# Mixture-of-experts layers: 32 slots for each of four experts side by side in TensorE's array, with a conditional block for ranks 32 to 63

## The chip, the cores and the metric

The kernel runs on one core of a Trainium2 chip, as one launch. The metric is the device time of that launch in microseconds, the median of several runs. A profile is one execution of the same program, taken by the hardware profiler.

## The reference, cut to what matters

The program is a DeltaNet layer and a product-key expert layer (the first block), then a second block of two layers. Each of the two layers is a token mixer followed by a mixture of experts. All of it is float32 on 256 tokens of 1024 channels. Only the mixture of experts is touched here. With `N_EXPERTS` = 32, `D_EXPERT` = 256 and `TOP_K` = 2 it is:

```python
def hierarchical_moe(h, w_grp, b_grp, w_exp, b_exp, w_gate, w_up, w_down):
    ...
    combine = jnp.einsum('tk,tke->te', weights,
                         jax.nn.one_hot(expert_id, N_EXPERTS, dtype=jnp.float32)).astype(t.dtype)
    y = jnp.zeros_like(t)
    for gi in range(N_GROUPS):
        sl = slice(gi * EXPERTS_PER_GROUP, (gi + 1) * EXPERTS_PER_GROUP)
        hid = jax.nn.silu(jnp.einsum('td,edf->tef', t, w_gate[sl])) * jnp.einsum('td,edf->tef', t, w_up[sl])
        y = y + jnp.einsum('tef,efd->td', hid * combine[:, sl, None], w_down[sl])
    return y.reshape(b, l, d)
```

A token goes to two of the eight experts of one group, so that 512 pairs of token and expert are spread over 32 experts. The reference evaluated on its inputs spreads them unevenly. In quads of four neighbouring experts, the fullest expert of each quad has 41, 35, 14, 11, 28, 31, 14 and 18 tokens in the first of the two layers, and 28, 25, 22, 30, 21, 12, 15 and 23 in the second.

## The kernel before, in words

`moe` (called once a layer) normalises the tokens, routes them and computes for each token and expert a rank `R`: the number of earlier tokens that chose the same expert, or a negative number where the token did not choose it. `cnt` holds the number of tokens of each expert. `moe_round` then computes all 32 experts for the tokens of ranks 0 to 63. If an expert had more than 64 tokens, a loop at the end of `moe` (L1793 to L1797) would run `moe_round` again with `R` lowered by 64.

`moe_round` works by pairs of experts (p = 0 to 15), 64 slots for each:

- `dispatch(q)`, once for each four experts: VectorE builds the selection matrix `sel` (256 tokens by 4 x 64 slots) from `R`, and TensorE multiplies the tokens (split into a high and a low part, `xh` and `xl`) with it (L1893, L1894), 32 matmuls of 256 columns. ScalarE and VectorE move the result to `xe`.
- `gate_up(p, k0)`: gate and up projection of the pair in one PSUM bank `pg`, L1914. Each of the two experts occupies 64 of the array's 128 columns, and streams its own weights `wgu` (512 columns).
- `turn(p)`: transposes of `sel` and of the hidden values `hs` (L1928, L1930).
- `down(p)`: the down projection with the weights `wdn` (L1946) into the banks `pw`, again two experts side by side; then the gate of the layer (L1951) and the split into `dsh` and `dsl` (L1952, L1953).
- `scatter(p)`: adds the pair to the tokens' accumulators `macc` (L1959).

The loop at the end of `moe_round` lays these out as a software pipeline: between the two halves of `gate_up(p)` comes `turn(p - 1)`, and `scatter(p - 2)` and `down(p - 1)` follow. TensorE takes its instructions in the order in which the tile library's scheduler put them, and so does each other engine.

The weights are the bulk of the traffic. An expert has four `wgu` tiles and two `wdn` tiles of 512 KB each. There is room for six experts (`units`, pools `mw` and `mw2`). Experts 0 to 3 are loaded during the token mixer, 4 and 5 at the start of `moe` (L1748), and the other 26 by SyncE's queue from inside the round (L1874): each load waits there, in order, until the matmuls that read the buffer's last content are done, and until the eighth load before it has landed.

The lines of the round:

Of the kernel before, what the change touches and what calls it, by code (L numbers as in the profile page):

```python
# [33 lines left out]
class Ker:  # L34
# [1229 lines left out]
    def units(self, e, part):  # L1264


        pool = self.mw2 if e % 6 > 3 or self.again else self.mw
        n = 2 if part else 4
        r = []
        for u in range(n):  # L1270
            for j in range(2):
                if part:
                    t = pool.tile([128, D], F32, name="wdn", bufs=8 if pool is self.mw else 4)
                    src = self.a["w2_d"][self.layer, e + j][:, u, :]
                else:
                    t = pool.tile([128, 2, 512], F32, name="wgu", bufs=16 if pool is self.mw else 8)
                    src = self.a["w2_gu"][self.layer, e + j][:, 2 * u:2 * u + 2, :]
                self.wt[e + j, part, u] = t
                yield t[:], src

# [456 lines left out]
    def moe(self, l):  # L1737
# [44 lines left out]
        self.moe_round(l, xh, xl, R, W, gc, sh, wk, 6, weights)  # L1782

        mx = sp.tile([128, 1], F32, name="mx")
        nr = sp.tile([128, 1], mybir.dt.int32, name="nr")
        nc.vector.tensor_reduce(mx[:], cnt[:], mybir.AxisListType.X, ALU.max)
        nc.vector.tensor_scalar(mx[:], mx[:], -1.0, None, ALU.add)
        nc.vector.tensor_copy(nr[:], mx[:])
        nc.vector.tensor_scalar(nr[:], nr[:], 6, None, ALU.arith_shift_right)
# [3 lines left out]
        n = nc.values_load(nr[0:1, 0:1], min_val=0, max_val=3)  # L1793
        with tc.For_i(0, n, 1):  # L1794
            nc.vector.tensor_scalar(R[:], R[:], -64.0, None, ALU.add)
            self.again = True
            self.moe_round(l, xh, xl, R, W, gc, sh, wk, 0)  # L1797
# [56 lines left out]
    def moe_round(self, l, xh, xl, R, W, gc, sh, wk, loaded, weights=None):  # L1854
# [9 lines left out]
        iota = self.sm("iota")[:, 0:64].unsqueeze(1).to_broadcast([128, 4, 64])  # L1864
        wt = self.wt

        room = 2 if self.again else 6
        ahead = [self.units(e, part) for e in range(loaded, room, 2) for part in range(2)]
        xe, sel, wsl, sT, hT, ds, hs, gu, nxt = [{} for _ in range(9)]
        bank = lambda: pw.tile([128, 512], F32, name="pw")  # L1870

        def load(n, it):
            for u in itertools.islice(it, n):
                nc.sync.dma_start(*u)  # L1874

        def later(e, part):
            return self.units(e, part) if e < 32 else iter(())

        def dispatch(q):

            sel[q] = wk.tile([128, 2, 4, 64], F32R, name="sel")
            for i in range(2):
                nc.vector.tensor_tensor(sel[q][:, i], iota, R[:, i, 4 * q:4 * q + 4].unsqueeze(2).to_broadcast([128, 4, 64]),
                                        ALU.is_equal)
            if weights and q == 0:
                weights()
            xe[q] = xp.tile([128, KC, 256], F32, name="xe")
            for k in range(KC):
                ps = bank()
                ks = slice(k * 128, (k + 1) * 128)  # L1890
                for i in range(2):
                    r = sel[q][:, i].rearrange("p e s -> p (e s)")
                    mm(ps[:, 0:256], xh[:, i, ks], r, start=i == 0, stop=False)  # L1893
                    mm(ps[:, 0:256], xl[:, i, ks], r, start=False, stop=i == 1)  # L1894
                if k % 2:
                    nc.scalar.activation(xe[q][:, k, :], ps[:, 0:256], AF.Identity, bias=sh[:, k:k + 1], scale=gc[:, k:k + 1])
                else:
                    nc.vector.tensor_scalar(xe[q][:, k, :], ps[:, 0:256], gc[:, k:k + 1], sh[:, k:k + 1], ALU.mult, ALU.add)
            ps = bank()
            for e in range(4):  # L1900
                for i in range(2):
                    mm(ps[e % 2 * 64:e % 2 * 64 + 64, e // 2:e // 2 + 1], sel[q][:, i, e, :].bitcast(F32),
                       W[:, i, 4 * q + e:4 * q + e + 1], start=i == 0, stop=i == 1)
            wsl[q] = wk.tile([128, 2], F32, name="wsl")
            nc.vector.tensor_copy(wsl[q][:], ps[:, 0:2])

        def gate_up(p, k0):
            if k0 == 0:
                nxt[p] = later(2 * p + room, 0)
                gu[p] = pg.tile([128, 512], F32, name="pg")  # L1910
            for k in range(k0, k0 + 4):
                for j in range(2):
                    s0 = (p % 2 * 2 + j) * 64
                    mm(gu[p][j * 64:j * 64 + 64, :], xe[p // 2][:, k, s0:s0 + 64], wt[2 * p + j, 0, k // 2][:, k % 2, :],  # L1914
                       start=k == 0, stop=k == KC - 1)
                if k % 2:
                    load(2, nxt[p])
            if k0:
                hs[p] = wk.tile([128, 256], F32, name="hs", bufs=1)
                nc.scalar.activation(hs[p][:], gu[p][:, 0:256], AF.Silu)  # L1920
                nc.vector.scalar_tensor_tensor(hs[p][:], hs[p][:], wsl[p // 2][:, p % 2:p % 2 + 1], gu[p][:, 256:512],
                                               ALU.mult, ALU.mult)

        def turn(p):
            tp = pw.tile([128, 4, 128], F32, name="pw")
            for i in range(2):
                s = sel[p // 2][:, i, p % 2 * 2:p % 2 * 2 + 2, :].rearrange("p e s -> p (e s)")
                nc.tensor.transpose(tp[:, 2 + i, :], s.bitcast(F32), self.ident)  # L1928
            for f in range(2):
                nc.tensor.transpose(tp[:, f, :], hs[p][:, f * 128:(f + 1) * 128], self.ident)  # L1930
            hT[p] = wk.tile([128, 2, 128], F32, name="hTs", bufs=1)
            nc.scalar.activation(hT[p][:], tp[:, 0:2, :], AF.Copy)
            sT[p] = wk.tile([128, 2, 128], F32R, name="sT")
            nc.vector.tensor_copy(sT[p][:], tp[:, 2:4, :])

        def down(p):
            ds[p] = [wk.tile([128, D], F32R, name=n, bufs=1) for n in ("dsh", "dsl")]
            if p == 15:

                pool = self.mw2 if self.again else self.mw  # L1940
                last = pool.tile([128, D], F32, name="wdn", bufs=4 if self.again else 8)
            for n in range(2):
                ps = bank()
                for f in range(2):
                    for j in range(2):
                        mm(ps[j * 64:j * 64 + 64, :], hT[p][:, f, j * 64:j * 64 + 64],  # L1946
                           wt[2 * p + j, 1, f][:, n * 512:(n + 1) * 512], start=f == 0, stop=f == 1)

                d = [t[:, n * 512:(n + 1) * 512] for t in ds[p]]
                t = last[:, n * 512:(n + 1) * 512] if p == 15 else wk.tile([128, 512], F32, name="dt", bufs=1)[:]  # L1950
                nc.vector.tensor_mul(t, ps[:], self.gt[:, n * 512:(n + 1) * 512])  # L1951
                nc.scalar.activation(d[0], t, AF.Copy)  # L1952
                nc.vector.tensor_tensor(d[1], t, d[0].bitcast(F32), ALU.subtract)  # L1953

        def scatter(p):
            for i in range(2):
                for n in range(2):
# [144 lines left out]
```

## Time and profile before

| what | value |
|---|---|
| time, median of 3 runs (lowest to highest) | 2340.88 us (2340.37 to 2342.99) |
| the profiled execution's own time | 2338.56 us |
| its span, from first to last instruction | 2336.8 us |
| TensorE (PE) busy | 2199.0 us, 94% |
| VectorE (DVE) busy | 1492.7 us, 64% |
| ScalarE (ACT) busy | 871.6 us, 37% |
| GpSimd (POOL) busy | 302.0 us, 13% |
| moved by DMA | 497.63 MB, mean 213 GB/s |
| first layer's round, first matmul of `dispatch` to last of `scatter` | 1581.1 to 1862.4 us |
| second layer's round, the same | 2043.8 to 2324.3 us |

The busy share is an average over stages with different limits, so the two rounds are to be read apart from the rest. Times in rows are microseconds from the start of the span. A row of TensorE is a hardware instruction: a float32 matmul of the program is issued as two of them, a matmul with the `fp32r` type as one. The granted clock is 1.00 at 2.4 GHz and 0.50 at 1.2 GHz.

### The profile page before, as it was taken

How to read it: one execution, taken by the hardware profiler on the slowest of the kernel's cores; microseconds unless marked ns; L12 is line 12 of the kernel's file. 1: busy time of each engine (PE TensorE's matmuls, PEld its weight loads, DVE VectorE, ACT ScalarE, POOL GpSimd, SP SyncE). 2: the span in 40 equal slices, each digit the busy share in tenths (PEclk: the TensorE clock that was granted, in tenths of full speed). 3: DMA queues.
4: the chain of work that ended last, by engine and by line, in shares of the span. 5: the costliest groups of instructions: out<-in, count | busy, mean ns of one | idle time of the engine just before them, and what ended most of it. 6: DMA issues, size and time to landing. Idle time of an engine off the chain costs nothing. (4 is left out here: it accounts for less than half of the span.)

```text
span 2336.8 us, 37643 instructions
## 1 busy us (share of the span) xinstructions
PE 2199.0 (94%) x14244; PEld 1602.3 (69%) x14244; DVE 1492.7 (64%) x3037; ACT 871.6 (37%) x1761; POOL 302.0 (13%) x354
## 2 busy tenths in 40 slices
PE   7889999998999999999999999989999899899997
PEld 4555667767999999998888878664443377644442
DVE  4787583356999999976666678773332387723223
ACT  3434434434445554444333343352111244421111
POOL 2533222232000000000000013230000032400000
PEclk9999897899999999999999999998999999999999
DMA  7576464465545444366555546638998167489971
GB/s 270 172 222 211 141 205 152 152 208 177 178 170 181 142 149 141 136 207 208 189 189 188 182 160 232 230 117 337 409 395 311 64 230 244 154 325 409 395 272 65
DMA packets 201762, 497.63 MB, mean 213 GB/s; under 512 B 16960, under 2 KB 84032, under 8 KB 200032
## 3 DMA queue, kind: packets, MB, share of 16 engines
q1 hardware_dynamic: 201568, 495.09, 60.3%
q8 instruction: 116, 1.90, 0.3%
q14 instruction: 78, 0.64, 0.1%
HBM read 492.86 MB, written 2.16 MB: 212 GB/s over the span
## 5 line engine op out<-in xcount | busy, mean ns | idle before, releaser
L52 PE MATMUL hps<-ph,esh 128*128 128x256 f32 x1152 | 332.8, 289 | 4.7 <-ACT esh L44 4.1
L54 PE MATMUL hps<-ph,esl 128*128 128x256 f32 x1152 | 329.0, 286 | 3.8 <-DVE esl L46 3.5
L53 PE MATMUL hps<-pl,esh 128*128 128x256 f32 x1152 | 326.3, 283 | 1.2 <-POOL pl L188 1.2
L44 ACT ACTIVATE esh<-x 128x1024 fp32r<-128x1024 f32 x170 | 180.3, 1060 | 277.4 <-PE y L54 122.0
L1914 PE MATMUL pg<-wgu,xe 128*64 128x512 f32 x1024 | 276.5, 601 | 0.0
L46 DVE TENSOR_TENSOR esl<-x,esh 128x1024 fp32r<-128x1024 f32 x170 | 206.9, 1217 | 55.1 <-ACT esh L44 53.1
L54 PEld LDWEIGHTS hps<-ph,esl 128*128 128x128 f32 x1152 | 220.4, 191 | 8.4 <-DVE esl L46 8.0
L52 PEld LDWEIGHTS hps<-ph,esh 128*128 128x128 f32 x1152 | 220.7, 192 | 5.9 <-ACT esh L44 4.3
L53 PEld LDWEIGHTS hps<-pl,esh 128*128 128x128 f32 x1152 | 220.9, 192 | 1.8 <-POOL pl L188 1.4
L53 PE MATMUL y<-esl,ech 128*128 128x512 f32 x512 | 202.0, 395 | 0.0
L54 PE MATMUL y<-esh,ecl 128*128 128x512 f32 x512 | 202.0, 394 | 0.0
L52 PE MATMUL y<-esh,ech 128*128 128x512 f32 x512 | 201.8, 394 | 0.0
L1914 PEld LDWEIGHTS pg<-wgu,xe 128*64 128x64 f32 x1024 | 79.0, 137 | 131.8 <-issue 124.9
L44 ACT ACTIVATE esh<-raw 128x1024 fp32r<-128x1024 f32 x92 | 97.6, 1061 | 149.3 <-PE y L54 71.9
L46 DVE TENSOR_TENSOR esl<-raw,esh 128x1024 fp32r<-128x1024 f32 x92 | 112.0, 1218 | 30.3 <-ACT esh L44 30.3
L46 DVE TENSOR_TENSOR wrsl<-wr,wrsh 128x512 fp32r<-128x512 f32 x135 | 108.3, 817 | 33.3 <-ACT wrsh L44 32.2
L1946 PE MATMUL pw<-wdn,hTs 128*64 128x512 f32 x512 | 124.1, 597 | 0.0
L44 ACT ACTIVATE wrsh<-wr 128x512 fp32r<-128x512 f32 x137 | 84.6, 628 | 86.6 <-PE pj L54 61.2
L107 PE MATMUL adaps<-adaw,cst 128*32 128x256 f32 x1024 | 91.8, 410 | 21.4 <-DMA adaw<-in_w_ada_dram 14.7
L54 PEld LDWEIGHTS y<-esh,ecl 128*128 128x128 f32 x512 | 96.4, 188 | 22.5
L53 PEld LDWEIGHTS y<-esl,ech 128*128 128x128 f32 x512 | 96.4, 188 | 22.1 <-DVE esl L46 0.3
L52 PEld LDWEIGHTS y<-esh,ech 128*128 128x128 f32 x512 | 96.5, 189 | 22.0 <-ACT esh L44 0.2
(612 smaller groups left out, 4556.3 us busy)
## 6 DMA issues: line engine op xcount, KB each, us to landing
wgu<-in_w_gu_dram SPq DMA_DIRECT2D x256, 512.0 KB
wdn<-in_w_d_dram SPq DMA_DIRECT2D x128, 512.0 KB
adaw<-in_w_ada_dram SPq DMA_DIRECT2D x96, 512.0 KB
x<-in_peer_u_dram SPq DMA_DIRECT2D x85, 512.0 KB
x<-in_peer_v_dram SPq DMA_DIRECT2D x75, 512.0 KB
raw<-in_peer_u_dram SPq DMA_DIRECT2D x43, 512.0 KB
raw<-in_peer_v_dram SPq DMA_DIRECT2D x43, 512.0 KB
dw<-in_dn_w_dram SPq DMA_DIRECT2D x64, 256.0 KB
```

The costliest lines, as they stand in the source:

```text
L44: nc.scalar.activation(hi[:], raw, AF.Copy)
L46: e.tensor_tensor(lo[:], raw, hi[:].bitcast(F32), ALU.subtract)
L52: mm(out, L[0], R[0], start=first, stop=False)
L53: mm(out, L[0], R[1], start=False, stop=False)
L54: mm(out, L[1], R[0], start=False, stop=last)
L107: nc.tensor.matmul(ps[g * 32:(g + 1) * 32, u * 256:u * 256 + 256], self.cst[:, which, k, :], wt[:, g, :], start=k + u == 0, stop=k + u == KC)
L1914: mm(gu[p][j * 64:j * 64 + 64, :], xe[p // 2][:, k, s0:s0 + 64], wt[2 * p + j, 0, k // 2][:, k % 2, :], start=k == 0, stop=k == KC - 1)
L1946: mm(ps[j * 64:j * 64 + 64, :], hT[p][:, f, j * 64:j * 64 + 64], wt[2 * p + j, 1, f][:, n * 512:(n + 1) * 512], start=f == 0, stop=f == 1)
```

## The change

`moe_round` works by quads of four experts (q = 0 to 7), with 32 slots for each, side by side in the array's 128 columns. `dispatch` gathers the tokens of eight experts at once. The software pipeline is gone: `experts` does gate and up, transposes, down and the split of one quad one after the other, and `scatter` follows. For each quad, a register is loaded with the number of tokens by which the quad's fullest expert exceeds 32 (`over`), and a block that is executed where it is positive does the quad once more for ranks 32 to 63, with a `dispatch` of its own for four experts. By the routing above the block is executed twice, for quads 0 and 1 of the first layer. The loop at the end of `moe` is for ranks from 64 on. The loads of experts 4q + 6 to 4q + 9 stand behind quad q; the six experts' room is as before.

```diff
+        def counts():
+            nc.vector.tensor_reduce(m4[:], cnt[:].rearrange("p (q e) -> p q e", e=4), mybir.AxisListType.X, ALU.max)
...
+            nc.vector.tensor_scalar(m4[:], m4[:], 32.0, 0.0, ALU.subtract, ALU.max)
+            nc.vector.tensor_copy(self.over[:], m4[:])
...
+        self.moe_round(l, xh, xl, R, W, gc, sh, wk, weights, counts)
...
-        def dispatch(q):
-
-            sel[q] = wk.tile([128, 2, 4, 64], F32R, name="sel")
+        def dispatch(e0, ne, r0, tag):
+
+            iota = self.sm("iota")[:, r0:r0 + 32].unsqueeze(1).to_broadcast([128, ne, 32])
+            sel = wk.tile([128, 2, ne, 32], F32R, name="sel" + tag, bufs=1 if tag else 2)
...
+            w = ne * 32
+            xe = (wk if tag else xp).tile([128, KC, w], F32, name="xe" + tag, tag="dsh" if tag else "xe", bufs=1)
...
+                    mm(ps[:, 0:w], xh[:, i, ks], r, start=i == 0, stop=False)
+                    mm(ps[:, 0:w], xl[:, i, ks], r, start=False, stop=i == 1)
...
+        def experts(q, sel, xe, wsl, c):
+
+            s0 = c * 128
+            gu = pg.tile([128, 512], F32, name="pg")
+            for u in range(4):
+                for k in range(2 * u, 2 * u + 2):
+                    for e in range(4):
+                        mm(gu[e * 32:e * 32 + 32, :], xe[:, k, s0 + e * 32:s0 + e * 32 + 32], wt[4 * q + e, 0, u][:, k % 2, :],
+                           start=k == 0, stop=k == KC - 1)
...
+            hs = wk.tile([128, 256], F32, name="hs", bufs=1)
+            nc.scalar.activation(hs[:], gu[:, 0:256], AF.Silu)
+            nc.vector.scalar_tensor_tensor(hs[:], hs[:], wsl[:, c:c + 1], gu[:, 256:512], ALU.mult, ALU.mult)
...
+            pd = [bank() for _ in range(2)]
+            for n, f in ((0, 0), (1, 0), (0, 1), (1, 1)) if again else ((0, 0), (0, 1), (1, 0), (1, 1)):
+                for e in range(4):
+                    mm(pd[n][e * 32:e * 32 + 32, :], hT[:, f, e * 32:e * 32 + 32],
+                       wt[4 * q + e, 1, f][:, n * 512:(n + 1) * 512], start=f == 0, stop=f == 1)
...
-        for it in ahead:
-            load(8, it)
-        dispatch(0)
-        for p in range(18):
-            if p < 16:
-                gate_up(p, 0)
-            if 1 <= p < 17:
-                turn(p - 1)
-            if p < 16:
-                gate_up(p, 4)
-                if p % 2 and p < 15:
-                    dispatch(p // 2 + 1)
-            if p >= 2:
-                scatter(p - 2)
-            if 1 <= p < 17:
-                down(p - 1)
-                load(4, later(2 * p - 2 + room, 1))
+        for q in range(8):
...
+            if q % 2 == 0:
+                P = dispatch(4 * q, 8, 0, "")
+            if q == 0:
+                scatter(*experts(q, *P, 0), True, False)
+            if not again:
+                v = nc.values_load(self.over[0:1, q:q + 1], min_val=0, max_val=224)
+                with tc.If(v > 0, preferred_fallthrough_block=False):
+                    scatter(*experts(q, *dispatch(4 * q, 4, 32, "2"), 0), False, False)
+            if q:
+                scatter(*experts(q, *P, q % 2), False, q == 7)
+            if not again:
+                for e in (4 * q + 6, 4 * q + 8):
+                    if e < 32:
+                        for part in range(2):
+                            load(self.units(e, part))
```

The order of instructions on two engines, at the two places that matter. On TensorE, in the first layer, from the end of the first `dispatch` on; before, the second pair's projections and transposes stand between those of the first:

```order
L1902 MATMUL pw<-Wc,sel 64x1 x8
L1914 MATMUL pg<-wgu,xe 64x512 x19
L1928 MATMUL pw<-masks,sel 128x128 x2
L1930 MATMUL pw<-masks,hs 128x128 x2
L1914 MATMUL pg<-wgu,xe 64x512 x8
```

In the change, in the same place, quad 0 runs through to its scatter:

```order
L1918 MATMUL pw<-Wc,sel 32x1 x16
L1931 MATMUL pg<-wgu,xe 32x512 x27
L1941 MATMUL pw<-masks,sel 128x128 x2
L1943 MATMUL pw<-masks,hs 128x128 x2
L1952 MATMUL pw<-wdn,hTs 32x512 x16
L1969 MATMUL macc_17225<-dsh,sT 128x512
L1969 MATMUL macc_17227<-dsh,sT 128x512
```

Six more accumulations of the scatter follow, and then the register load and the branch of quad 0 (L1981, L1982). What moved: nothing of another quad stands any more between a quad's projections, its transposes, its down projection and its scatter.

On SyncE, in the first layer, the loads of experts 4 and 5 (L1748) and those that follow, before:

```order
L1748 DMA wgu<-in_w_gu_dram 128x1024 x8
L1748 DMA wdn<-in_w_d_dram 128x1024 x4
L1874 DMA wgu<-in_w_gu_dram 128x1024 x16
L1874 DMA wdn<-in_w_d_dram 128x1024 x4
L1874 DMA wgu<-in_w_gu_dram 128x1024 x8
```

and in the change, behind the loads of experts 4 and 5 (now L1760) and the register loads for all eight quads, which stand together; the last register here is the one of the loop at the end:

```order
L1813 TENSOR_LOAD nr
L1813 ISA x2
L1982 COMPARE_AND_BRANCH
L1982 UNCONDITIONAL_BRANCH x2
L1890 DMA wgu<-in_w_gu_dram 128x1024 x8
L1890 DMA wdn<-in_w_d_dram 128x1024 x4
L1890 DMA wgu<-in_w_gu_dram 128x1024 x2
L1982 COMPARE_AND_BRANCH
```

What moved: the first load of expert 6 stands behind quad 0's branch. The first two loads of a buffer that the block of quad 0 may read wait for TensorE's semaphore at a count inside that block (its projections), the `wdn` loads for one in its down projection. Where the block is not executed, TensorE waits for its own count at the end of quad 0's scatter and then raises the semaphore by the block's whole 100 at once. Each engine takes its branch by itself; none waits for another one there. The loads of later quads wait for matmul after matmul of the quad before, as in the kernel before.

## Rows read from the trace of the kernel before

**Rows 1.** The page's first part: busy time, share of the span and instructions of each engine.

```profile
PE 2199.0 (94%) x14244; PEld 1602.3 (69%) x14244; DVE 1492.7 (64%) x3037; ACT 871.6 (37%) x1761; POOL 302.0 (13%) x354
```

**Rows 2.** Windows of the rounds: stretch, length, engines' busy us (count), clock, DMA, GB/s.

```profile
1581.10:1862.40 281.30, 276.59 (x1344) 125.04 (x1344) 83.44 (x166) 51.95 (x98) 2.51 (x5) 0.98 0.80 306
2043.80:2324.30 280.50, 275.78 (x1344) 124.29 (x1344) 83.41 (x166) 51.90 (x98) 0.00 (x0) 0.99 0.79 303
1640.00:1700.00 60.00, 60.00 (x318) 28.02 (x316) 19.25 (x36) 11.69 (x22) 0.00 (x0) 1.00 1.03 408
1805.00:1862.00 57.00, 55.20 (x237) 21.40 (x236) 16.09 (x28) 9.50 (x18) 2.51 (x5) 1.00 0.16 55
```

**Rows 3.** Groups by line, first layer's round: busy us, mean ns of one.

```profile
L1914 PE MATMUL pg<-wgu,xe 128*64 128x512 f32 x512 | 138.2, 601 | 0.0
L1946 PE MATMUL pw<-wdn,hTs 128*64 128x512 f32 x256 | 62.0, 597 | 0.0
```

**Rows 4.** SyncE's timeline, first layer: start, us, the loads issued.

```profile
1570.24 4.65 SPq L1748 DMA_DIRECT2D wgu<-in_w_gu_dram  x8
...
1590.81 17.09 SPq L1874 DMA_DIRECT2D wgu<-in_w_gu_dram  x16
...
1795.19 26.01 SPq L1874 DMA_DIRECT2D wdn<-in_w_d_dram  x8
```

**Rows 5.** The page's part on DMA issues: count and size of the experts' loads, both layers.

```profile
wgu<-in_w_gu_dram SPq DMA_DIRECT2D x256, 512.0 KB
wdn<-in_w_d_dram SPq DMA_DIRECT2D x128, 512.0 KB
```

**Rows 6.** TensorE's timeline, matmuls of four 32-column tiles side by side: start, us.

```profile
51.66 1.07 PE L322 MATMUL adaps<-adaw,cst 128*32 128x256 f32 x16
...
64.52 0.64 PE L107 MATMUL adaps<-adaw,cst 128*32 128x256 f32 x8
```

**Rows 7.** TensorE's timeline, both rounds: `dispatch`, start of the projections, ends.

```profile
1581.12 0.55 PE L1893 MATMUL pw<-sel,xh 128*128 128x256 f32 x1 [1.10 <-DVE sel L1883]
...
1591.04 0.28 PE L1893 MATMUL pw<-sel,xh 128*128 128x256 f32 x1
1591.16 0.28 PE L1894 MATMUL pw<-sel,xl 128*128 128x256 f32 x1
...
1593.19 8.83 PE L1914 MATMUL pg<-wgu,xe 128*64 128x512 f32 x38
...
1602.23 0.38 PE L1930 MATMUL pw<-masks,hs 128*128 128x128 f32 x2
...
1856.55 2.79 PE L1946 MATMUL pw<-wdn,hTs 128*64 128x512 f32 x10
...
1861.76 0.63 PE L1959 MATMUL macc<-dsl,sT 128*128 128x512 f32 x2
...
2055.07 8.83 PE L1914 MATMUL pg<-wgu,xe 128*64 128x512 f32 x38
...
2323.69 0.62 PE L1959 MATMUL macc<-dsl,sT 128*128 128x512 f32 x2
```

**Rows 8.** Timelines of ScalarE and VectorE behind the first pair's projections.

```profile
1598.63 0.38 ACT L1920 ACTIVATE hs<-pg 128x256 f32<-128x256 f32 x1 [4.82 <-PE pg L1914]
1599.05 0.48 DVE L1921 SCALAR_TENSOR_TENSOR hs<-hs,wsl,pg 128x256 f32<-128x256 f32 x1 [5.46 <-ACT hs L1920]
1602.65 0.39 ACT L1932 ACTIVATE hTs<-pw 128x256 f32<-128x256 f32 x1 [3.64 <-PE pw L1930]
```

**Rows 9.** Register load and branches of the loop at the end: ns min/median/max.

```profile
L1793 PEldq TENSOR_LOAD <-nr x2: 316/402/488, 1861.5 to 2323.4; - x2
L1794 PEldq COMPARE_BRANCH  x6: 82/190/3617, 1862.2 to 2329.1; - x6
```

**Rows 10.** Windows with the granted clock where TensorE waits, and behind it.

```profile
1573.00:1581.00 8.00, 0.81 (x10) 0.60 (x9) 6.76 (x32) 4.83 (x10) 4.26 (x4) 0.68 0.98 353
1581.00:1590.00 9.00, 8.23 (x28) 5.84 (x30) 4.32 (x19) 1.33 (x3) 0.00 (x0) 0.52 0.94 375
```

More of the change, by code (lines that the diff above doesn't have):

```diff
@@ L1279, in units, with unit4 @@
                 yield t[:], src
+    def unit4(self, q, part, u):
+        for e in range(4 * q, 4 * q + 4):
+            if part:
+                t = self.mw2.tile([128, D], F32, name="wdn", bufs=4)
+                src = self.a["w2_d"][self.layer, e][:, u, :]
+            else:
+                t = self.mw2.tile([128, 2, 512], F32, name="wgu", bufs=8)
+                src = self.a["w2_gu"][self.layer, e][:, 2 * u:2 * u + 2, :]
+            self.wt[e, part, u] = t
+            yield t[:], src
     def mixer(self, l):
@@ L1897, in dispatch @@
                 else:
[L1898 removed]
+                    nc.vector.tensor_scalar(xe[:, k, :], ps[:, 0:w], gc[:, k:k + 1], sh[:, k:k + 1], ALU.mult, ALU.add)
             ps = bank()
[L1900 removed]
+            for e in range(ne):
                 for i in range(2):
[L1902 to L1903 removed]
@@ L1904, in dispatch @@
[L1904 to L1922, printed above, removed]
@@ L1931, in turn @@
[L1931 to L1941, printed above, removed]
-            for n in range(2):
[L1943 to L1953, printed above, removed]
@@ new lines, in experts, with scatter @@
+            for n in range(2):
+                d = [t[:, n * 512:(n + 1) * 512] for t in ds]
+                t = wk.tile([128, 512], F32, name="dt", bufs=1)
+                nc.vector.tensor_mul(t[:], pd[n][:], self.gt[:, n * 512:(n + 1) * 512])
+                nc.scalar.activation(d[0], t[:], AF.Copy)
+                nc.vector.tensor_tensor(d[1], t[:], d[0].bitcast(F32), ALU.subtract)
+            return sT, ds
+        def scatter(sT, ds, first, last):
+            for n in range(2):
+                for i in range(2):
+                    for h in range(2):
+                        mm(acc[2 * i + n][:], sT[:, i, :], ds[h][:, n * 512:(n + 1) * 512],
+                           start=first and h == 0, stop=last and h == 1)
@@ new lines, in moe_round @@
+        for q in range(8):
+            if again:
+                for u in range(2):
+                    load(self.unit4(q, 0, u))
+                load(self.unit4(q, 1, 0))
+            if q % 2 == 0:
[13 more added lines that the diff above has]
+                            load(self.units(e, part))
```

75 lines of the change are left out of this document (38 added, 37 removed).

## The prediction

> **What bounds the kernel now.** I read the page first: TensorE is busy for 94% of the span [rows 1], so it seems to set the pace everywhere. The change touches only the two rounds of experts, so I went on to windows of those. In each of them TensorE is busy for 276 of 281 us, at a granted clock of 0.98 to 0.99 [rows 2]. DMA is not far behind. From 1640 to 1700 it moves 408 GB/s at a share of 1.03, the most that it holds over a long stretch, while from 1805 to 1862 it has almost nothing left to do (55 GB/s) [rows 2]. So two limits lie close together: the array sets the end of a round, and in its middle the weights arrive no faster than they are used. The question is what is left when the array's work shrinks: the stream of weights, and when it may run.
>
> **The array's work.** Gate and up take 138.2 us and down 62.0 us of the first round [rows 3], with two experts side by side. Four tiles of 32 columns side by side are in this trace elsewhere: 16 instructions of 256 columns take 1.07 us, 8 take 0.64 us [rows 6], so eight more cost 0.43 us, 0.054 us each, and one of 512 columns costs 0.107 us by that. A quad has 64 such instructions in gate and up (6.8 us) and 32 in down (3.4 us). What used to stand beside other pairs' work is now in the open. Between gate and up and the transposes of `hs` lie ScalarE's and VectorE's steps, 1598.63 to 1599.53, with a semaphore some 1.0 us [rows 8]; transposes and their copy take from 1602.23 to 1603.04, 0.8 us [rows 7, 8]. From the end of the last down (1859.34) to the end of the last scatter (1862.39) it is 3.05 us [rows 7], which holds the split on VectorE and ScalarE. A `dispatch` for eight experts has the same 32 matmuls of 256 columns as one for four had; they start 0.12 us apart [rows 7], 3.8 us, about 5 us with its evacuations, 2.5 us a quad. Register load and branch: 0.4 us and 0.2 us at the median, and from 0.4 to 4.1 us between the ends [rows 9]; those rows are of one place, where the engines stood still. I take 0.6 us. Sum: 6.8 + 1.8 + 3.4 + 3.05 + 2.5 + 0.6 = 18 us a quad.
>
> **The weights.** A quad has 24 tiles of 512 KB, 12.6 MB, 30.8 us at 408 GB/s. That is longer than 18 us, so DMA becomes the bound, if it is fed. With room for six experts, the two that are not in the running quad are on their way while it runs, and two more follow into the buffers that its gate and up gives back matmul by matmul. From the moment the last pair's first tiles arrive, DMA has some 28 us of work that is already released, and the quad gives its `wgu` buffers back within 10 us and its `wdn` buffers within 20 us. So it stays fed. Then a round lasts until the loads may start, plus their whole time, plus the work behind the last of them. There are 256 + 128 loads in two layers [rows 5], 192 in each, 36 of which are issued ahead; 156 are left, 81.8 MB, 200.5 us at 408 GB/s [rows 2].
>
> **When the loads start.** Before, the first of the 156 was issued at 1590.81 [rows 4], in the middle of the first pair. In the change the buffers of experts 0 to 3 are also read by quad 0's conditional block, so those loads wait for it, or for the branch past it. Here DMA will idle, and this is what the gain is reduced by.
>
> Second layer (no block executed): `dispatch` ends as before, its 32 matmuls are the same, and the remaining gate and up starts at 2055.07 [rows 7]. 27 matmuls, two instructions each, 5.8 us; then 1.8, 3.4 and 3.05 us: the scatter ends at 2069.2, with the branch 2070. I add 3 us until the queue is full, an estimate between nothing and the 4.65 us that issuing eight loads takes [rows 4]. The last tile lands at 2070 + 3 + 200.5 = 2273.5. Behind it are three quarters of a down, 2.6 us, and the 3.05 us: 2279 against 2324.3 [rows 7], **45 us less**.
>
> First layer: the scatter of quad 0 ends at 1593.19 + 14.05 = 1607.2 [rows 7]. Its block is executed (41 tokens): branch and `sel` 1.3 us, a `dispatch` of 32 matmuls of 128 columns, for which there is no row of that kind; I take the 0.12 us of the 256-column ones as its upper end (half of it as its lower) and 5.2 us with the evacuations; gate and up 6.8 us. The loads start at 1620.5. Quad 1's block (35 tokens) comes before quad 1 itself and delays the release of experts 4 and 5: block 0 ends at 1628.8, block 1 (21.5 us) at 1650.3, and the first tile of quad 1 is free at about 1653, when DMA, with 30.8 us of released work, is just about to run dry (1654). I put 2 us there. 1620.5 + 3 + 200.5 + 2 + 5.6 = 1831.6 against 1862.4, **31 us less**.
>
> Other edits: `counts` does seven small VectorE instructions, in place of four that were there already and in gaps of `dispatch`; nothing, and 1 us at each start if a gap is missed. SyncE's nine register loads (some 0.5 us each by [rows 9]) stand behind the loads of experts 4 and 5 while it has only to wait for quad 0; if that cover were gone they would cost 5 us. The loop at the end and the mixers are as before.
>
> Sum: 45 + 31 = 76 us off the profiled execution's own 2338.56 us, 2262.6. The median of the runs is 2.3 us above that execution, so 2265 us.
>
> **The clock.** Where TensorE waited before the round (0.81 us busy of 8) the granted clock is 0.68, and in the 9 us behind it, 8.23 us of them busy, it is 0.52, the 1.2 GHz level [rows 10]. In the change the array waits for some 12 us of each quad's 30.8 us, so I expect quads to begin at the low level. Half speed for 9 us costs a quad some 4.5 us, 22.5 us in place of 18, still under 30.8. The Trainium skill, TensorE: Matmul & The Clock Gate, section HAM oscillation — how this bites in real kernels, says that where a step's compute is shorter than its wait for data, the array falls back in every wait and every step starts cold. That speaks against the change, and the rows just named agree with it for one wait; cold starts alone would leave the sum where it is, as the 22.5 us show, but for 2 to 3 us behind the last tile of a round. What would change it is an array that never gets back to 2.4 GHz, the first rival.
>
> **The rivals.**
>
> *The array stays at 1.2 GHz* (slower). The prices: gate and up 13.7, the steps to down 2.2, down 6.8, what follows 4.2, `dispatch` 4.5, branch 0.6, 32 us a quad: over 30.8 us, from where on the array decides. Second layer: 2055.07 + 24.7 + 7 x 32 = 2304, 20 us less. First layer: two blocks of 36.4 us more, 1593.19 + 24.7 + 73 + 224 = 1915, 53 us more. Together 2374 us. For it: the long waits. Against it: in [rows 10] work alone brought the clock back, and the round is at 0.98 [rows 2]. Chance 0.05.
>
> *DMA runs dry in every quad.* Four of six experts' buffers are held by the running quad, and SyncE issues in order. With 5 us of idle DMA for six quads of each layer, 60 us are given back: 2325 us. Against it: the 28 us of released work. Chance 0.10.
>
> *Four tiles of 512 columns go no faster than two.* Then gate and up takes 13.7 and down 6.8 us, and a quad 28 us, still under DMA; but quad 0, the two blocks and the ends get longer by some 45 us in all: 2310 us. Against it [rows 6]. Chance 0.04.
>
> *No block is executed*, because the kernel's routing stays at 32: the first layer saves 45 us as well, 2251 us. Chance 0.03.
>
> **How the numbers follow.** The forecast has 0.78. Its own bounds: branches at 4.1 us, one on the second layer's way and three on the first's, +14 us; blocks partly at 1.2 GHz, +15 us; without the 3 us of filling and the 2 us at quad 1, -8 us. That is 2252 to 2295. To hold eight of ten the range goes from 2250, which takes in the rival without blocks, to 2305. About 0.2% (5 us) is what a measurement of this kernel can tell from no change. Faster: all but the first rival and a part of the second, 0.92; within 0.2%: 0.02; slower: 0.06.
>
> **What would show it.** Right: windows of a round at over 400 GB/s from some 18 us (second layer) or 30 us (first) behind the row where gate and up starts [rows 7] until a few us before its end; TensorE's busy share there down to some 60%; matmuls of L1931 0.11 us apart where they don't wait; 128-column `dispatch` matmuls twice in the first layer and nowhere in the second. Wrong: gaps in the DMA windows between quads, TensorE busy all the time at a clock of 0.5, or a first load well behind 2071.

## The result, and the profile after

The change takes the kernel from 2341.64 us to 2269.86 us (medians of four runs each; 2263.41 to 2276.92 after). The ratio is 0.9694, 95% interval 0.9663 to 0.9725. The profiled execution took 2267.36 us, 71.2 us less than that of before.

TensorE's row of the page, which answers to [rows 1]: 2199.0 us busy have become 2017.3.

```profile
PE 2017.3 (89%) x14108; PEld 1505.6 (66%) x14108; DVE 1420.7 (63%) x2919; ACT 828.6 (37%) x1681; POOL 301.9 (13%) x354
```

Windows of the kernel after, columns as in [rows 2]: both rounds, the long stretch of the second, two where the loads of the first begin, three at its quad 1, two with waits, and the stretch ahead of the first loads in each.

```profile
1585.30:1836.40 251.10, 195.48 (x1428) 81.00 (x1428) 53.80 (x117) 33.60 (x64) 2.51 (x5) 0.90 0.87 344
2017.90:2255.30 237.40, 167.16 (x1120) 66.77 (x1120) 44.35 (x96) 27.81 (x53) 0.00 (x0) 0.86 0.90 358
2046.00:2236.00 190.00, 127.60 (x850) 50.70 (x854) 30.30 (x56) 18.92 (x36) 0.00 (x0) 0.84 1.02 411
1610.00:1620.00 10.00, 9.47 (x85) 5.61 (x88) 2.32 (x8) 1.83 (x4) 0.00 (x0) 1.00 0.07 20
1620.00:1630.00 10.00, 8.90 (x76) 2.75 (x68) 2.23 (x4) 1.40 (x3) 0.00 (x0) 1.00 0.55 163
1630.00:1650.00 20.00, 17.79 (x143) 8.39 (x146) 4.64 (x12) 3.22 (x7) 0.00 (x0) 1.00 1.03 408
1650.00:1660.00 10.00, 9.28 (x72) 3.04 (x68) 2.77 (x4) 1.26 (x2) 0.00 (x0) 1.00 0.82 310
1660.00:1680.00 20.00, 17.38 (x159) 8.45 (x149) 6.59 (x13) 4.28 (x8) 0.00 (x0) 1.00 1.01 375
1750.00:1760.00 10.00, 3.54 (x14) 1.23 (x18) 0.00 (x0) 0.00 (x0) 0.00 (x0) 0.61 1.02 410
1810.00:1820.00 10.00, 3.53 (x9) 0.56 (x13) 0.00 (x0) 0.00 (x0) 0.00 (x0) 0.51 1.03 415
2022.00:2045.00 23.00, 20.00 (x160) 8.16 (x158) 6.19 (x15) 5.00 (x8) 0.00 (x0) 0.93 0.07 27
1593.00:1618.00 25.00, 22.62 (x209) 10.68 (x211) 6.67 (x15) 6.27 (x11) 0.00 (x0) 1.00 0.01 5
```

The limit has changed hands. In the second round DMA moves 411 GB/s for 190 us on end while TensorE is busy for 67% of them; before, TensorE was busy for 98% of a round at 303 to 306 GB/s [rows 2]. What is left of the old picture is ahead of the first loads: 23 to 25 us in each round in which DMA moves next to nothing (27 and 5 GB/s).

SyncE's timeline after, answering to [rows 4] (start, us, the loads issued): the first loads of the 156 in each layer, the late ones of quad 1, and the last.

```profile
1618.07 9.64 SPq L1890 DMA_DIRECT2D wgu<-in_w_gu_dram  x8
1657.02 6.18 SPq L1890 DMA_DIRECT2D wgu<-in_w_gu_dram  x8
2043.98 5.03 SPq L1890 DMA_DIRECT2D wgu<-in_w_gu_dram  x8
2233.39 5.00 SPq L1890 DMA_DIRECT2D wdn<-in_w_d_dram  x4
```

TensorE's timeline after, answering to [rows 7]: the first `dispatch` of each round, the projections behind it, quad 0's scatter and quad 1's projections.

```profile
1585.34 0.55 PE L1909 MATMUL pw<-sel,xh 128*128 128x256 f32 x1 [1.10 <-DVE sel L1897]
1595.45 6.21 PE L1931 MATMUL pg<-wgu,xe 128*32 128x512 f32 x54
1610.09 0.74 PE L1969 MATMUL macc<-dsl,sT 128*128 128x512 f32 x2
1655.08 7.07 PE L1931 MATMUL pg<-wgu,xe 128*32 128x512 f32 x64
2017.90 0.55 PE L1909 MATMUL pw<-sel,xh 128*128 128x256 f32 x1 [1.10 <-DVE sel L1897]
2028.48 6.21 PE L1931 MATMUL pg<-wgu,xe 128*32 128x512 f32 x54
2043.12 0.74 PE L1969 MATMUL macc<-dsl,sT 128*128 128x512 f32 x2
2051.51 8.81 PE L1931 MATMUL pg<-wgu,xe 128*32 128x512 f32 x60 [7.66 <-issue]
```

A round is measured here from its first `dispatch` matmul to VectorE's first addition to `x`. VectorE's timeline, before (L1987) and after (L2000):

```profile
1861.38 2.70 DVE L1987 TENSOR_TENSOR x<-x,macc 128x512 f32<-128x512 f32 x4
2323.31 2.70 DVE L1987 TENSOR_TENSOR x<-x,macc 128x512 f32<-128x512 f32 x4
```

```profile
1836.40 1.27 DVE L2000 TENSOR_TENSOR x<-x,macc 128x512 f32<-128x512 f32 x2
1838.87 1.29 DVE L2000 TENSOR_TENSOR x<-x,macc 128x512 f32<-128x512 f32 x2 [0.59 <-PE macc L1969]
2252.19 1.28 DVE L2000 TENSOR_TENSOR x<-x,macc 128x512 f32<-128x512 f32 x2
2254.66 1.28 DVE L2000 TENSOR_TENSOR x<-x,macc 128x512 f32<-128x512 f32 x2 [0.59 <-PE macc L1969]
```

The first round went from 280.3 to 251.1 us (-29.2), the second from 279.5 to 234.3 (-45.2). This measure serves to compare the change with its variants. Against the kernel before it flatters the change by 1.7 us a round: there the four additions follow one another, here the last two wait for the end of the scatter. To the end of the last scatter product, the point to which the prediction counts, the rounds go from 281.3 to 253.7 us (-27.5; the end is at 1839.07) and from 280.5 to 237.0 (-43.5; 2254.86), together -71.0. Against that, the first `dispatch` starts 4.2 us later than in [rows 7], behind the same instructions; the stretches behind the two rounds are 4.4 us shorter. That start lies between 1573.3 and 1592.3 in the profiles below, whose programs are alike ahead of the rounds but for the zero products of three of them. So small effects are read from the rounds here, and the medians stand beside them.

### The profile page after: what moved, and what is told of

It reads as the page before. It is cut to its first block, busy times and chain, and to the rows that moved or that the text cites. A ratio compares the mean times of both kernels' runs of the same rounds, so it can differ in the third digit from the quotient of the medians.

```text
span 2265.6 us, 37317 instructions
## 1 busy us (share of the span) xinstructions
PE 2017.3 (89%) x14108; PEld 1505.6 (66%) x14108; DVE 1420.7 (63%) x2919; ACT 828.6 (37%) x1681; POOL 301.9 (13%) x354
## 3 DMA queue, kind: packets, MB, share of 16 engines
q8 instruction: 133, 2.18, 0.4%
## 5 line engine op out<-in xcount | busy, mean ns | idle before, releaser
L1931 PE MATMUL pg<-wgu,xe 128*32 128x512 f32 x1152 | 182.8, 678 | 90.7 <-DMA wgu<-in_w_gu_dram 46.7
L52 PEld LDWEIGHTS hps<-ph,esh 128*128 128x128 f32 x1152 | 221.2, 192 | 5.3 <-ACT esh L44 3.8
L1931 PEld LDWEIGHTS pg<-wgu,xe 128*32 128x32 f32 x1152 | 50.8, 121 | 204.8 <-issue 102.2
L1937 DVE SCALAR_TENSOR_TENSOR hs<-hs,wsl,pg 128x256 f32<-128x256 f32 x18 | 8.6, 479 | 211.6 <-ACT hs L1936 211.6
```

Source lines behind the costliest of these rows:

```text
L52: mm(out, L[0], R[0], start=first, stop=False)
L1931: mm(gu[e * 32:e * 32 + 32, :], xe[:, k, s0 + e * 32:s0 + e * 32 + 32], wt[4 * q + e, 0, u][:, k % 2, :], start=k == 0, stop=k == KC - 1)
L1937: nc.vector.scalar_tensor_tensor(hs[:], hs[:], wsl[:, c:c + 1], gu[:, 256:512], ALU.mult, ALU.mult)
```

## The experiments

Theory A is the prediction's: a round is the start of its first loads, plus the loads at DMA's rate, plus a short tail, and TensorE has room to spare. Its rival B: TensorE's chain of a quad, with a branch that can take 6 us, sets the pace, and DMA keeps just ahead. What made B worth testing is TensorE's wait of 7.66 us above and these rows of the kernel after: all branches (ns min/median/max), those of the second layer's quads 0 and 1, the queue of instructions in the DMA from 2043.2 to 2052, with quad 1's long branch, and from 1779 to 1789, with quad 6's (packets, MB, share). (`PEldq` is the part of TensorE that takes its weight loads and its branches, as the rows have it.)

```profile
L1982 PEldq COMPARE_BRANCH  x30: 64/226/6132, 1610.7 to 2223.6; - x30
L1982 PEldq COMPARE_BRANCH  x4: 70/206/6132, 2043.5 to 2045.1; - x4
q8 instruction: 2, 0.03, 1.8%
q8 instruction: 1, 0.02, 0.7%
```

Seven of the 14 times that a block is passed over, TensorE's branch takes 4.5 to 6.1 us. Inside each of these seven the queue of instructions moves a packet of 16 KB between the weights (two in quad 1's; 133 of them make 2.18 MB on the page), and the branch ends 1.4 to 1.5 us behind the last; inside the seven short ones there is none. So the long branches are waits for instructions. The Trainium skill, Runtime: NRT & Kernel Launch, section Instruction fetch mechanics, says that a taken branch to code outside the small window of fetched pages has to fetch it by DMA first. The rows agree with it: a 16 KB packet in each of the seven. A full DMA alone does not make a branch long: the one into block 1 (1632.7) took 0.21 us while DMA moved 408 GB/s. Nor does an idle DMA make it free: the longest of [rows 9], at 1862.58, took 3.6 us while DMA moved 7 GB/s, with one such packet in it.

All runs (rounds are those of one profile each). The kernel before, run again beside the variants, has medians of 2340.87 to 2345.01 us and single runs from 2324.51 to 2351.27:

| run | median us | first round | second round |
|---|---|---|---|
| before | 2341.64 | 280.3 | 279.5 |
| the change | 2269.86 | 251.1 | 234.3 |
| no_block | 2222.48 | 222.3 | 221.2 |
| if_q01 | 2268.48 | 255.1 | 234.4 |
| block_first | 2260.77 | 259.7 | 225.5 |
| fewer_loads | 2210.15 | 229.2 | 211.6 |
| gu2 | 2317.26 | 284.1 | 250.0 |
| gu4 | 2454.41 | 353.5 | 316.9 |
| pairs | 2263.77 | 251.3 | 234.7 |
| fallthrough | 2271.83 | 251.3 | 235.6 |
| gu2_if01 | 2269.95 | 250.0 | 234.6 |
| pairs8 | 2263.19 | 250.9 | 235.0 |
| warm | 2270.28 | 252.9 | 235.0 |
| mid_warm | 2250.22 | 247.5 | 222.7 |

**no_block**: the branch and the block under it are gone.

```diff
-            if q == 0:
-                scatter(*experts(q, *P, 0), True, False)
-            if not again:
...
-            if q:
-                scatter(*experts(q, *P, q % 2), False, q == 7)
+            scatter(*experts(q, *P, q % 2), q == 0, q == 7)
```

> Leaves out the tokens of ranks 32 to 63 (the conditional blocks and their branches are gone). Theory A (the round is the start of the first loads, plus 156 loads of 512 KB at about 408 GB/s, plus a short tail): the first loads now follow the first gate/up rows of quad 0 instead of block 0 or the scatter, so they start about 21 us earlier in the first layer (1597 instead of 1618) and 18 us earlier in the second (2026 instead of 2044), and the stretch of thin DMA at quad 1 of the first layer (about 5 us) goes: -44 us, 2226 us (2218 to 2234). Theory B (TensorE's own chain per quad, branches included, sets the pace): two blocks of about 22 us and seven long branches of about 6 us go: -85 us, 2185 us.

Measured: 2222.48 us, -47 against the change. The first loads come 9.8 and 9.2 us behind the first `dispatch` (1583.09 and 1990.12), where they came 32.7 and 26.1 us behind it:

```profile
1583.09 7.04 SPq L1890 DMA_DIRECT2D wgu<-in_w_gu_dram  x8
1990.12 7.25 SPq L1890 DMA_DIRECT2D wgu<-in_w_gu_dram  x8
```

The rounds are 28.8 and 13.1 us shorter, 41.9 against A's 44, with the second layer gaining 5 us less and the first 3 us more than I had put. The second layer did not turn all of its 16.9 us into time: from 2002 to 2010 DMA moved 306 GB/s. B's 85 us did not come.

**if_q01**: `if not again:` becomes `if not again and q < 2:`.

> The conditional block stands for quads 0 and 1 only; the six later ones of each layer, which this input never enters, are gone with their branches. Of the seven TensorE branches of 4.5 to 6.1 us, six go. Theory A: they lie beside loads that bound the round, so nothing changes: 2270 us (2262 to 2277). Theory B (TensorE's chain sets the pace): six times about 6 us go, 2234 us.

2268.48 us; the second round is 234.4 us, as with the branches. So the six long branches that are gone cost this kernel nothing: they lie in TensorE's waits for weights. (The seventh, ahead of quad 1 of the second layer, stays. The first round is 4 us longer; TensorE's clock was at 0.53 in its first block, from 1610 to 1620, and at 1.00 with the change.)

**fewer_loads**: eight experts of a layer take over tiles.

```diff
-                    if e < 32:
+                    if e < 32 and e % 6 > 3 and e > 4:
...
+                                    wt[e + j, part, u] = wt[e + j - 6, part, u]
+                    elif e < 32:
```

> Eight experts of each layer (10, 11, 16, 17, 22, 23, 28, 29) read the tiles of the expert six before them and are not loaded: 48 of the 156 loads of a layer after the first 36 are gone, 25.2 MB or 61.7 us at 408 GB/s. All products still run. Theory A: the round falls until TensorE bounds it. With 18 us a quad and 3 us of branch on average, seven quads from quad 1's main gate/up (1655, 2051) take 147 us, so the first layer ends near 1803 instead of 1835 and the second near 2199 instead of 2254: -88 us, 2182 us (2170 to 2205). Theory B: TensorE sets the pace already, 2265 to 2270 us.

2210.15 us, 60 of A's 88 us: the sign and most of the size are A's. (The profiled execution, 2221.01 us, is the slowest of the four; its rounds give 44.6 us.) The first round gains 21.9 us, not 32: quad 1 begins 4 us later behind the first `dispatch` than in the change, as in if_q01, and TensorE takes over at 22 us a quad, not 21 (seven quads from 1654 to 1810, in which the trace names a load as the end of no wait, and DMA moves 294 GB/s). In the second, one more block was executed: the scatter's row of this run has 76 products of each kind, four for each pass, so 19 passes and not 18 (other weights in the first layer give another routing in the second). That is some 22 us of TensorE's time.

```profile
L1969 PE MATMUL macc<-dsh,sT x76: 388/446/504, 1602.2 to 2207.0; 128*128 128x512 f32 x76
```

**gu2** and **gu4**: each product of gate and up in quads 2 to 6 is done two or four times, the sum scaled back (the edit of gu2; gu4 has 4 for 2).

```diff
+            n = 2 if 1 < q < 7 and not again else 1
...
-                    for e in range(4):
...
+                    for t in range(n):
+                        for e in range(4):
...
-            nc.scalar.activation(hs[:], gu[:, 0:256], AF.Silu)
+            nc.scalar.activation(hs[:], gu[:, 0:256], AF.Silu, scale=1.0 / n)
```

> Quads 2 to 6 of both layers run their gate and up products twice (10 quads, 6.9 us more TensorE work each). Theory A: the loads bound these quads (30.8 us of DMA against some 18 us of TensorE work and up to 4 us of branch), so the added work lies in waits: 2270 us (2262 to 2278), and the DMA keeps over 400 GB/s. Theory B (TensorE's chain sets the pace): +69 us, 2339 us.

> The same four times (20.6 us more in each of 10 quads). A quad now takes some 41.5 us of TensorE, over the 30.8 us of its loads. Theory A, with the point where TensorE takes over: five quads of 41.5 us from quad 2's start (1676 and 2075), then quad 7 in 18 us: the layers end near 1902 and 2300 instead of 1836 and 2254, +113 us, 2383 us (2350 to 2410). Theory B: four times 6.9 us, +206 us, 2476 us.

2317.26 and 2454.41 us: both far over A, below B. A's mechanism survives only with another size: with doubled products a quad is already over its 30.8 us. TensorE's waits in gu2 from 1690 to 1876 (us in total, times, longest) show why: seven of 3.9 to 6.6 us, with a branch of 5.0 to 6.3 us in each of the five quads from 1700 to 1862.

```profile
PE pg L1933 <- issue: 22.2, 4, 6.6
PE pg L1933 <- DMA wgu<-in_w_gu_dram: 12.9, 2, 6.6
PE pg L1933 <- SPq L1814: 6.4, 1, 6.4
```

DMA, at 411 GB/s in the change, is no longer the bound there (window of gu2, columns as above):

```profile
1690.00:1860.00 170.00, 126.01 (x992) 42.53 (x988) 23.71 (x43) 14.66 (x28) 2.50 (x5) 0.87 0.96 359
```

The five quads from 1689 to 1859 take 34 us each: 25.5 us of products and steps, the share of a `dispatch`, and the branch. In gu4 it is 48 us, from 1684 to 1925, with branches of 5.6 to 7.1 us; A had 41.5, and ten quads of 6.6 us more make 66 of the 71 us by which A missed.

**gu2_if01**: gu2 and if_q01 together.

> Quads 2 to 6 run their gate and up products twice, as in the run before, and the six conditional blocks that this input never enters are gone with their branches. Theory F (TensorE's branch past a block that isn't entered waits some 6 us while weight loads fill the DMA engines; with the doubled products it was these waits that put a quad over the 30.8 us of its loads): a quad takes 25.5 us plus 3 us of dispatch, under 30.8, and most of the 47 us goes: 2272 us (2262 to 2285). Theory G (the doubled products are over the loads by themselves): 2317 us (2305 to 2325).

2269.95 us, as F said: all of the 47 us are gone. The same waits in this run, from 1690 to 1834, and a window of it:

```profile
PE pg L1933 <- DMA wgu<-in_w_gu_dram: 6.1, 5, 5.1
PE pw L1945 <- DVE hs L1939: 5.6, 6, 1.0
1690.00:1790.00 100.00, 93.18 (x742) 34.27 (x746) 20.02 (x37) 12.24 (x23) 0.00 (x0) 1.00 1.03 413
```

The edit does two things at once, it takes away the waits and it lets the next quad's products begin between the steps of this one; the 41.5 us of waits in gu2's rows are more than the 33 us by which its first round grew, so the waits alone are enough for it, but how much the other did was not measured. With the branches the change's own room is small: gu2's products, 8 to 9 us longer, put a quad 3 us over its 30.8, which leaves between 5 and 6 us, not the 12 that I counted. This is an estimate from gu2's first layer, and a low one, for in each layer gu2 has a long branch in three quads more than the change.

**fallthrough**: `preferred_fallthrough_block=True`.

> The conditional block's code stands the other way round (the block's side of the branch is the one that falls through). If the 4 to 6 us of seven of TensorE's branches come from a jump over code that isn't taken, they move to another place or go; theory A hides them on either side: 2270 us (2262 to 2278). Theory B: 2235 us if the long ones go, the same if they only move.

2271.83 us, rounds as with the change. TensorE still has branches of up to 6.1 us in this form. Since the long branches stayed, the run does not tell A from B.

**pairs** and **pairs8** (the edit of pairs; in pairs8 the loop over `g` stands outside of that over `u`): in quads 2 to 6 two experts' products alternate, within each tile of weights (pairs) or over all of an expert's eight (pairs8). A product is two of TensorE's instructions, so a row of the trace counts twice as many.

```diff
-                for k in range(2 * u, 2 * u + 2):
-                    for e in range(4):
...
+                for g in ((0, 1), (2, 3)) if 1 < q < 7 and not again else ((0, 1, 2, 3),):
+                    for k in range(2 * u, 2 * u + 2):
+                        for e in g:
...
```

> In quads 2 to 6 the gate and up products go by two experts at a time (two 32-column tiles in turn, not four). If products of different column tiles overlap in the array, these rows stand 0.21 us apart instead of 0.11 and a quad takes 6.9 us more, which theory A hides beside the loads: 2270 us (2262 to 2278). If four tiles were no faster than two, the spacing stays 0.11 us, with the same time. Theory B with overlap: +69 us, 2339 us.

> In quads 2 to 6 the first two experts run all 16 of their gate and up products before the other two begin, so that products for the other columns can't step in between. If four column tiles side by side are worth twice two, a group of products costs as in the doubled run: a quad takes 6.9 us more and the time is that run's, 2317 us (2300 to 2330). If two tiles are as fast as four: 2270 us (2262 to 2278).

`pairs` does not tell two tiles from four: its products ran as fast as in the change. TensorE's rows at quad 2, of the change and of `pairs`:

```profile
1676.28 3.63 PE L1931 MATMUL pg<-wgu,xe 128*32 128x512 f32 x29 [0.72 <-PEq L1982]
```

```profile
1673.52 3.63 PE L1932 MATMUL pg<-wgu,xe 128*32 128x512 f32 x29 [0.73 <-PEq L1983]
```

In `pairs8`, where the 16 products of two experts (32 instructions) stand in a row, quad 2 takes 12.52 us for the 64 instructions that took 7.07 us in quad 1 of the change:

```profile
1671.34 12.52 PE L1932 MATMUL pg<-wgu,xe 128*32 128x512 f32 x64 [0.73 <-PEq L1983]
```

So four column tiles side by side run 1.8 times as fast as two. The time did not go to 2317 us as I expected from gu2, it is 2263.19: a quad's 5.5 us more still fit into the room, and one of the four branches from 1700 to 1810 was short (0.3 us), where gu2 had five long ones.

**block_first**: the block goes ahead of the main quad in quad 0 too; products with a zero tile start the accumulators.

```diff
-            if q == 0:
-                scatter(*experts(q, *P, 0), True, False)
+            if q == 0 and not again:
...
+                for t in acc:
+                    mm(t[:], self.USb[:], z[:], start=True, stop=False)
...
-            if q:
-                scatter(*experts(q, *P, q % 2), False, q == 7)
+            scatter(*experts(q, *P, q % 2), q == 0 and again, q == 7)
```

> In quad 0 the block goes ahead of the main projections, as in the other quads; four products with a zero tile start the accumulators. Theory A: in the second layer, where no block runs, the loads follow the first gate/up rows of quad 0 rather than its scatter. They started at 2044; they now start at 2031 if the branch is short and at 2037 if it takes the 6 us: -7 to -13 us there. In the first layer the PE work ahead of quad 1's main gate/up is the same, so 0 to +3 us. Sum -9 us, 2261 us (2255 to 2266). Theory B: the PE work per quad is the same, 2270 us.

The second round came as A said (-8.8 us, loads at 16.0 us behind the first `dispatch`), the first is 8.6 us longer, so the rounds say no gain. The median is 9 us lower. In the profiled execution the 6.4 us that it is ahead come from a first `dispatch` that starts 7.7 us earlier; that the medians differ by this alone is not shown. What the first round lost lies ahead of quad 1's projections, 77.8 us behind the first `dispatch` instead of 69.7, and a large part of it is the clock: windows of this run, with the block's `dispatch`, and the block's products behind them (62 instructions in 8.91 us, where the change has 61 in 7.06).

```profile
1590.00:1595.00 5.00, 5.00 (x18) 3.34 (x18) 0.82 (x2) 0.82 (x2) 0.00 (x0) 0.50 0.00 0
1595.00:1600.00 5.00, 5.00 (x43) 2.34 (x46) 0.57 (x2) 1.83 (x3) 0.00 (x0) 0.50 0.00 0
```

**warm**: such zero products, 20 of them, with the order of the change.

> Twenty products with a zero tile start and fill the accumulators; they have nothing to wait for, and ten stand in TensorE's wait ahead of the ranks, five ahead of the first dispatch and five in it. Theory A: TensorE's time ahead of the first loads counts one for one. If they keep the granted clock at 1.00, the first dispatch, which now runs at 0.50, takes some 4 us less in each layer: -8 us, 2262 us (2256 to 2268). If the clock falls in what is left of the wait, nothing changes: 2270 us.

2270.28 us: no gain, though the clock did what was wanted: 1.00 from 2013 to 2022, where the second layer's first `dispatch` stands. There the time from the ranks to the main run of gate and up fell from 12.0 to 9.4 us. It was given back behind it: ScalarE's table for Silu, which had been loaded while it waited, now loads when the products are done (ScalarE's timeline, with the wait ahead of it; the change, then `warm`), and the down projection, behind waits of 1.96 and 0.47 us, began at a clock of 0.50 (2032 to 2034) and took 5.03 us, not 3.64.

```profile
2028.87 1.28 ACT L1936 ACT_TABLE_LOAD   x1
```

```profile
2028.91 1.28 ACT L1936 ACT_TABLE_LOAD   x1 [5.92 <-PE pg L1931]
```

**mid_warm**: the zero products, and in quad 0 the branch right behind the main gate and up products.

```diff
-            if q == 0:
-                scatter(*experts(q, *P, 0), True, False)
...
+            gu = gate_up(0, *P, 0) if q == 0 else None
...
-            if q:
-                scatter(*experts(q, *P, q % 2), False, q == 7)
+            scatter(*experts(q, *P, q % 2, gu), q == 0 and again, q == 7)
```

> As the run with zero products, and in quad 0 the branch to the block stands right behind the main gate and up products, ahead of the rest of the main quad. Theory A: in the second layer the first loads then follow those products (some 8 us earlier); in the first layer the work ahead of quad 1's main gate/up is the same (0). With the warm clock -16 us, 2254 us (2246 to 2262); with the clock as before -8 us, 2262 us.

2250.22 us, ratio to before 0.9618 (0.9584 to 0.9652): faster than both kernels (the change's interval begins at 0.9663). The rounds are 3.6 and 11.6 us shorter than the change's. SyncE's first loads of each layer, 21.2 and 14.3 us behind the first `dispatch`:

```profile
1608.95 9.78 SPq L1890 DMA_DIRECT2D wgu<-in_w_gu_dram  x8
2029.27 4.52 SPq L1890 DMA_DIRECT2D wgu<-in_w_gu_dram  x8
```

In the second layer they are 11.8 us earlier and the round 11.6 us shorter: one for one. In the first they are 11.5 us earlier and only 3.6 are won, because quad 1, behind two blocks, still gives its tiles back 67 us behind the first `dispatch` (70 with the change): from 1650 to 1660 DMA moves 123 GB/s. What the zero products and the place of the branch give each was not measured in this run; the zero products alone gave nothing (warm).

## Why the prediction came out

The forecast was 2265 us against 2269.86, the change of the profiled execution -76 against -71.2, and the rounds, counted to the last scatter product, -31 and -45 against -27.5 and -43.5. The mechanism came out: a start of the loads, the loads at DMA's rate, a tail. That the total is within 5 us is in part luck, for terms of the first layer were off by 4 to 5 us in both directions. By its steps:

- **DMA becomes the bound.** Shown: 411 GB/s over 190 us, and taking a third of the loads away (fewer_loads) shortens the rounds, while TensorE's branches (if_q01) can go without effect. "So it stays fed" held in all quads but quad 1 of the first layer. Of the signs named, TensorE's busy share (67%) and the spacing of L1931 (64 in 7.07 us, 0.11 each) came; over 400 GB/s came some 5 us later behind the row of the projections than named (from 2052 and 1630).
- **When the loads start, second layer.** Predicted 14.9 us behind the row of the projections, measured 15.5; from there to the end of the scatter 209 us predicted (3 + 200.5 + 5.6), 210.9 measured (to 2254.86).
- **When the loads start, first layer.** I let the loads wait for the end of block 0's gate and up, 27.3 us behind that row; they begin with its first products, 22.6 us behind. These 4.7 us are lost again at once: the eight loads are issued over 9.64 us, and up to 1630 DMA moves 1.8 MB, 4.5 us of work in 12, so that filling the queue cost 7.4 us where I had 3. Quad 1's tiles came free later too: its projections start 59.6 us behind the row, and I had 57.1 for the end of block 1. The stretch at quad 1 cost DMA some 4 us (310 and 375 GB/s in the windows above, against 410) where I had put 2. From the row to the end it is 243.6 us, and I had 238.4. mid_warm shows that an earlier start alone gains little here: quad 1 binds.
- **The tail, 5.6 us.** I had three quarters of a down and the scatter behind the last tile. In the second layer the last load is issued at 2233.39 and DMA still moves 352 GB/s from 2244 to 2246; TensorE ends quad 7's gate and up at 2245.1, so that the transposes and a whole down stand behind it as well. From there it is 9.8 us to the end, in the first layer (1829.3) the same. In the second, DMA's 411 GB/s instead of 408 and a shorter filling give back about half of this.
- **18 us a quad.** Gate and up 7.07 (6.8), down 3.64 (3.4). Quad 1 with a whole `dispatch` and a short branch runs from 1655.08 to 1676.28, 21.2 us; I had 20.5 for such a quad.
- **The branch, 0.6 us.** This is the term that was furthest off: half of the times it is 4.5 to 6.1 us, above the upper end of 4.1 that [rows 9] gave. It cost nothing in the six quads that if_q01 covers, for which I had no reason but the room in the quad; by gu2 this room ends some 5 to 6 us further on.
- **Blocks.** Executed twice in the first layer, never in the second, as assumed. Their `dispatch` has 128-column matmuls 0.11 us apart (1611.22 and 1611.33, for two of them), about my upper end.
- **The clock.** It falls to 0.51 and 0.61 in slices with waits, and DMA stays at 410 to 415 GB/s there: harmless in the middle of a round, as said. The Trainium skill's page TensorE: Matmul & The Clock Gate, section HAM oscillation — how this bites in real kernels, tells of a loop whose compute is shorter than its wait for data, and has every step of it start cold. A quad here computes for longer than it waits; the clock is below 1.00 in eight of the 13 slices of 10 us from 1700 to 1830, and the time does not suffer, since the loads, not the array, end last. Ahead of the first loads it counts: block_first lost time there.
- **The rivals.** An array that stays at 1.2 GHz: the granted clock is at 0.84 on the mean of the 190 us, and back at 1.00 in five of those 13 slices. (That work brings it back is to be read from [rows 2], 0.98 over a round; [rows 10] ends at 0.52.) DMA dry in every quad: not seen. Four tiles no faster than two: pairs8 speaks against it. No block executed: two were.
- **The range.** The lower of its own bounds adds up to 2257 us (2265 less 8), not 2252; the range began at 2250 for another reason. And 0.2% was too little for what a measurement can tell: the change's four runs lie 13.5 us apart.

## What to carry to other kernels

When work on the bounding engine shrinks past the next limit, cost the stream behind it from the moment it may start: here, in the second layer, a microsecond by which the first loads came earlier was worth 0.8 to 1 (no_block, block_first, mid_warm), and less in the first, where another release bound. Place a conditional block so that what it holds back (buffers, loads) is held as short as it can be, and price the branch that skips it in the state it will run in, with DMA full, not from a place where everything stands still. And a change that saves time ahead of a step must be followed through that step: a table load or a falling clock can take it back.

## What had not been expected

- A branch past a block of code costs TensorE 4.5 to 6.4 us while weight loads run, seven of 14 times in the change and 13 of 14 in gu2; the others take 0.3 to 0.4 us. Each long one has an instruction packet inside it, and the loop's branch, with DMA at 7 GB/s, still took 3.6 us. In the change it is quads 4, 6 and 7 in both layers and quad 1 of the second, so the position of the code may have a part in it. What decides wasn't tried apart. Straight code seems to wait as well: three waits of 2.0 to 4.4 us inside a quad's projections (up to 1681.94, 1701.82 and 2080.37) end 1.2 to 1.5 us behind such a packet, with no branch in them; two of them the trace puts down to a load, so this is not shown.
- Products for other columns of the array start while earlier ones of the program's order still wait: past the four products of two experts (eight instructions) in `pairs`, where the third expert's first row starts 0.03 us behind the first's, but not past their 16 (32 instructions) in `pairs8`. (This takes the order of the source for the engine's.)
- Halving the columns of a `dispatch` matmul from 256 to 128 leaves its spacing at 0.11 against 0.12 us (1669.33 and 1669.45 for two of 256 columns).
